# Regrouping a masked-softmax matmul: one quarter of the rows of eight batches per group, in 16 KB runs, on one Trainium2 core

## The chip, the cores and the metric

The kernel runs on one core of one Trainium2 chip, the others being idle. The metric is device time in microseconds; shorter is better. An execution counts as fast or slow by its state (one that is over 1.5% above the fastest of the same kernel is called slow; a single run's state is unknown), and ratios use fast runs only. A profile's span is some 1.8 us shorter than the time of the same execution.

## The reference, cut to what matters

```python
batch, m, k, n = 16, 512, 512, 512          # x: 16 x 512 x 512 float32, weight: 512 x 512 float32
mask = np.triu(np.ones((m, n))) == 0        # 1 strictly below the diagonal
y = scale * np.matmul(x, weight)
y = np.where(mask == 1, y, -1e9)
y_max = np.max(y, axis=-1, keepdims=True)
y_exp = np.exp(y - y_max)
return y_exp / np.sum(y_exp, axis=-1, keepdims=True)
```

16.8 MB come in, 16.8 MB go out. The part of a row above the diagonal is zero in the result, so products there can be left out; row 0 is masked completely and comes out as 1/512 everywhere.

## The kernel before

A group is one half (256) of the rows of two neighbouring batches. A partition holds four neighbouring rows, 8 KB, as one run, in input and output. HBM side: 64 row sets (`p`) of 2 batches (`e`).

```python
x_r = x.rearrange("(c e) (h p t) k -> c h p e (t k)", e=2, h=2, t=T)        # T = 4
out_r = out.rearrange("(c e) (h p t) n -> c h p e (t n)", e=2, h=2, t=T)

def load(u):
    xf = x_pool.tile([P, T, K], FP32, name="xf")                            # 8 buffers
    seq(nc.sync.dma_start(xf.rearrange("p t k -> p (t k)"), x_r[u // 2, u % 2]))
# ... cast to bf16 (VectorE), 16 transposes (TensorE), eviction (VectorE and ScalarE) ...
def multiply(u):                                                            # cut
    NC = (h + 1) * HB                                                       # 256 or 512 columns
    for t in range(T):
        for kt in range(KT):
            seq(nc.tensor.matmul(py[:, :NC], lhsT=xt[:, kt, t], rhs=w_bf[:, kt, :NC], ...))
        seq(nc.tensor.matmul(py[:, h * HB : NC], lhsT=ident_bf, rhs=band[:, h, t], ...))   # adds the mask
        seq(nc.scalar.activation(out=ot[:, t, :NC], in_=py[:, :NC], func=AF.Exp, accum_out=...))
# ... normalise (VectorE) ...
def store(u):
    seq(nc.sync.dma_start(out_r[u // 2, u % 2], ot.rearrange("p t n -> p (t n)")))
```

`band` is the mask spread over the partitions by eight products and eight copies before the loop.

The softmax here doesn't subtract the row's maximum and nothing guards it: scores larger than these inputs give would overflow.

## Time and profile before

| | before |
|---|---|
| time, median of 4 runs | 90.53 us (90.43 to 90.63) |
| span of the profile | 88.8 us |
| moved | 34.87 MB in 37 transfers; 4224 packets of 8 KB, 512 of 512 bytes |
| TensorE busy | 71.3 us |

The main lines of this profile stand in the prediction. Beside them, these from the page's list of transfers (what is moved, queue, count, KB each, median us from issue to landing):

```profile
xf<-in_x_dram SPq DMA_DIRECT2D x16, 1024.0 KB, 13.7
out_dram<-ot SPq DMA_DIRECT2D x16, 1024.0 KB, 11.9
```

A load of 1 MB needs 2.5 us at 425 GB/s. That it lands 13.7 us after its issue means that it stands in a queue behind others. While such a queue stood, the 16 transfer engines were full: a share of 0.99 to 1.04 in the stretches from 12 to 85 us. (A packet is one record of the trace and here one run: 4224 of 8 KB are 33 transfers of 128 runs. The share of transfer time, below, is the time of the packets over that of 16 engines; a packet counts where it starts, so a stretch can pass 1.)

### The profile page before, as it was taken

What the parts mean: (1) busy time and instruction counts of PE and PEld (TensorE: products, weight loads), DVE (VectorE), ACT (ScalarE), POOL (GpSimd) and SP (SyncE); (2) the same over time, 40 slices, a digit from 0 to 9 for tenths busy, and PEclk for the clock granted to TensorE, in tenths of its full rate; (3) what the DMA queues carried; (4) which work ended last, traced back from release to release, by engine and by line L of the source; (5) the groups of instructions that cost most, each with busy time, mean ns of one, the idle gap of its engine ahead of it and who ended that gap; (6) DMA issues with size and microseconds to landing.
All of it is one profiled execution on the core that took longest, in us unless ns stands there. A gap on an engine that the chain in (4) does not pass through costs nothing.

```text
span 88.8 us, 1632 instructions
## 1 busy us (share of the span) xinstructions
PE 71.3 (80%) x596; PEld 49.3 (56%) x596; DVE 60.6 (68%) x124; ACT 55.2 (62%) x154; POOL 7.3 (8%) x20
## 2 busy tenths in 40 slices
PE   4984409999999999999999999999999999800000
PEld 1324109875795598479659857965895695300000
DVE  5866485479799779949986987976594998070000
ACT  5401461887797686969777787977778786710000
POOL 7620000002001000200010020002000202000000
PEclk9999655899999999999999999999999999997555
DMA  0899999999999999999999999999999999999970
GB/s 15 306 373 384 381 376 428 417 432 428 414 425 417 425 436 428 402 417 432 428 428 417 428 421 421 425 436 425 421 417 432 425 421 425 428 432 428 425 306 26
DMA packets 5334, 34.95 MB, mean 394 GB/s; under 512 B 592, under 2 KB 1104, under 8 KB 1104
## 3 DMA queue, kind: packets, MB, share of 16 engines
q1 hardware_dynamic: 5328, 34.87, 94.6%
q8 instruction: 4, 0.07, 0.3%
q14 instruction: 2, 0.02, 0.0%
HBM read 18.09 MB, written 16.78 MB: 393 GB/s over the span
## 4 chain that ended last, share of the span: by engine, by line
PE 72%; DMA 10%; DVE 3%; SPq 2%; ACT 1%; DVEq 0%; issue 0%; ACTq 0%
PE py L116 47%; PE pt L92 16%; DMA xf<-in_x_dram 10%; PE py L125 8%; DVE ot L152 1%; DVE xb L83 1%; SPq L163 1%; SPq L78 1%; ACT ot L135 1%; PE py L215 0%; SPq L167 0%; DVEq L284 0%; DVE rinv L150 0%; ACTq L284 0%
## 5 line engine op out<-in xcount | busy, mean ns | idle before, releaser
L116 PE MATMUL py<-w_bf,xt 128*128 128x256 bf16 (+1 forms) x256 | 50.0, 329 | 0.0
L135 ACT ACTIVATE ot<-py 128x256 f32<-128x256 f32 (+1 forms) x64 | 31.2, 493 | 7.5 <-PE py L125 7.1
L116 PEld LDWEIGHTS <-xt 128*128 128x128 bf16 x256 | 24.8, 99 | 12.2
L103 ACT COPY xt<-pt 128x1024 bf16<-128x1024 bf16 x16 | 16.2, 1012 | 12.9 <-PE pt L92 8.8
L152 DVE TENSOR_SCALAR ot<-ot,rinv 128x256 f32<-128x256 f32 (+1 forms) x64 | 23.5, 431 | 0.8
L83 DVE CAST xb<-xf 128x2048 bf16<-128x2048 f32 x16 | 19.5, 1220 | 5.0 <-DMA xf<-in_x_dram 5.0
L92 PE MATMUL pt<-ident_bf,xb 128*128 128x128 bf16 x256 | 17.8, 225 | 3.7 <-DVE xb L83 3.7
L92 PEld LDWEIGHTS <-xb 128*128 128x128 bf16 x256 | 16.6, 115 | 5.8 <-DVE xb L83 4.9
L125 PE MATMUL py<-band,ident_bf 128*128 128x256 bf16 x64 | 17.6, 275 | 0.0
L102 DVE COPY xt<-pt 128x1024 bf16<-128x1024 bf16 x16 | 11.0, 687 | 6.2 <-PE pt L92 6.2
L135 ACT ACTIVATION_READ_ACCUMULATOR ot<-py 128x1 f32 x64 | 12.8, 200 | 0.0
L154 POOL MEMSET ot<- 2x256 f32 x8 | 3.6, 448 | 65.7 <-DVE ot L152 65.7
L125 PEld LDWEIGHTS <-ident_bf 128*128 128x128 bf16 x64 | 6.3, 99 | 4.2
L180 PE MATMUL py<-zeros 128*128 128x512 bf16 x12 | 5.2, 619 | 1.2 <-DVE zeros L177 1.2
L150 DVE RECIPROCAL rinv<-rsum 128x4 f32<-128x4 f32 x16 | 2.7, 168 | 2.8 <-ACT ot L135 2.8
L186 DVE MEMSET ot<- 128x1024 f32 x4 | 3.6, 912 | 0.6 <-issue 0.6
L180 PEld LDWEIGHTS <-zeros 128*128 128x128 bf16 x12 | 1.6, 144 | 3.9 <-issue 2.8
L226 DVE CAST band<-py 64x256 bf16<-64x256 f32 x4 | 1.6, 414 | 2.5 <-PE py L215 2.5
L215 PE MATMUL py<-diag_bf,spread 128*128 128x256 bf16 x8 | 1.6, 339 | 1.2 <-DVE diag_bf L202 1.2
L226 ACT CAST band<-py 64x256 bf16<-64x256 f32 x4 | 1.4, 367 | 1.4 <-DVE band L226 1.4
L193 ACT ACT_TABLE_LOAD x1 | 1.3, 1283 | 0.7 <-PEq L270 0.7
L215 PEld LDWEIGHTS <-spread 128*128 128x128 bf16 x8 | 0.9, 111 | 1.5 <-issue 1.3
(14 smaller groups left out, 7.5 us busy)
## 6 DMA issues: line engine op xcount, KB each, us to landing
xf<-in_x_dram SPq DMA_DIRECT2D x16, 1024.0 KB, 13.7
out_dram<-ot SPq DMA_DIRECT2D x16, 1024.0 KB, 11.9
w_f<-in_weight_dram SPq DMA_DIRECT2D x1, 1024.0 KB, 7.0
diag_f<-in_mask_dram SPq DMA_DIRECT2D x4, 64.0 KB, 7.7
```

The costliest lines, as they stand in the source:

```text
L83: seq(nc.vector.tensor_copy(xb, st_x.pop(u)))
L92: nc.tensor.transpose(st_pt[u][kt // 2][:, kt % 2, t], xb[:, t].rearrange("p (k kt) -> p kt k", kt=KT)[:, kt], ident_bf,)
L102: seq(nc.vector.tensor_copy(xt[:, 0:2], pt[0]))
L103: seq(nc.scalar.copy(xt[:, 2:4], pt[1]))
L116: nc.tensor.matmul(py[:, :NC], lhsT=xt[:, kt, t], rhs=w_bf[:, kt, :NC], start=(kt == 0), stop=(kt == KT - 1),)
L125: nc.tensor.matmul(py[:, h * HB : NC], lhsT=ident_bf, rhs=band[:, h, t], start=False, stop=True, skip_group_check=True,)
L135: nc.scalar.activation(out=ot[:, t, :NC], in_=py[:, :NC], func=AF.Exp, bias=0.0, scale=float(scale), accum_out=rsum[:, t : t + 1],)
L152: seq(nc.vector.tensor_scalar_mul(ot[:, t, :NC], ot[:, t, :NC], rinv[:, t : t + 1]))
L154: seq(nc.gpsimd.memset(ot[0:2, 0, :HB], 1.0 / N))
L180: seq(nc.tensor.matmul(idle, lhsT=zeros[:, :P], rhs=zeros, start=True, stop=True))
L186: nc.vector.memset(ots[i][:, :, HB:], 0.0)
L226: seq(copy(band[half, h, t : t + 2, g * P : (g + 1) * P], src[half, :, g]))
```

## The change

Its intent: longer runs (16 KB) and fewer, larger transfers; products only up to the diagonal block of 128 columns; the mask block multiplied as loaded, through a matrix that picks its rows, in place of the spread `band`. The core of the diff, with cuts:

```diff
+S = 8
+T = 4
+X_BUFS = 5
...
-    x_r = x.rearrange("(c e) (h p t) k -> c h p e (t k)", e=2, h=2, t=T)
-    out_r = out.rearrange("(c e) (h p t) n -> c h p e (t n)", e=2, h=2, t=T)
+    x_r = x.rearrange("(c e) (q p t) k -> c q p e (t k)", e=E, q=Q, t=S)      # E = 8, Q = 4
+    out_r = out.rearrange("(c e) (q p t) n -> c q p e (t n)", e=E, q=Q, t=S)
...
-        NC = (h + 1) * HB
+        NC = (q + 1) * P
...
-                    py[:, h * HB : NC],
-                    lhsT=ident_bf,
-                    rhs=band[:, h, t],
+                    py[:, q * P : NC],
+                    lhsT=spread[:, slots(u)][:, t],
+                    rhs=diag_bf[:, q],
...
+            if g in (0, G - 1):
+                store(g, slots(u - 1))
+            elif part == R - 1:
+                store(g)
```

The HBM side of a transfer now has 16 row sets (`p`) of 8 batches (`e`). The loads of x and the stores share this shape.

More of the change, by code (lines that the diff above doesn't have):

```diff
@@ L15 @@
 P = 128
-X_BUFS = 8
-OUT_BUFS = 8
-WARM = 12
+S = 8
+T = 4
+X_BUFS = 5
 @with_exitstack
@@ L45 @@
     K2, N = weight.shape
-    assert K == K2 and N == 512 and K == 512 and M == 512 and B % 2 == 0
+    assert K == K2 and N == 512 and K == 512 and M == 512 and B % S == 0
     KT = K // P
-    T = 4
-    HP = P // 2
-    HB = 2 * P
-    U = B
+    E = S
+    Q = M // P
+    R = S // T
+    OUT_BUFS = 8 * T // S
+    G = B // E * Q
+    U = G * R
     const = ctx.enter_context(tc.tile_pool(name="const", bufs=1))
@@ L65, with quarter, slots, load @@
     w_bf = const.tile([P, KT, N], BF16, name="w_bf")
-    diag_f32 = const.tile([P, KT, P], FP32, name="diag_f32")
-    diag_bf = const.tile([P, KT, P], BF16, name="diag_bf")
-    spread = const.tile([P, T, P], BF16, name="spread")
+    diag_f32 = const.tile([P, Q, P], FP32, name="diag_f32")
+    diag_bf = const.tile([P, Q, P], BF16, name="diag_bf")
+    spread = const.tile([P, S, P], BF16, name="spread")
     zeros = const.tile([P, N], BF16, name="zeros")
-    band = const.tile([P, 2, T, HB], BF16, name="band")
-    ots = [const.tile([P, T, N], FP32, name=f"ot{i}") for i in range(OUT_BUFS)]
+    ots = [const.tile([P, S, N], FP32, name=f"ot{i}") for i in range(OUT_BUFS)]
     st_x, st_xb, st_pt, st_xt, st_sum = {}, {}, {}, {}, {}
     seq = tc.keep_in_program_order
-    def load(u):
-        xf = x_pool.tile([P, T, K], FP32, name="xf")
-        seq(nc.sync.dma_start(xf.rearrange("p t k -> p (t k)"), x_r[u // 2, u % 2]))
-        st_x[u] = xf
+    def quarter(g):
+        return Q - 1 - g % Q
+    def slots(u):
+        return slice(T * (u % R), T * (u % R) + T)
+    def load(g, part=slice(0, S)):
+        if g not in st_x:
+            st_x[g] = x_pool.tile([P, S, K], FP32, name="xf")
+        run = slice(part.start * K, part.stop * K)
+        seq(nc.sync.dma_start(st_x[g].rearrange("p t k -> p (t k)")[:, run], x_r[g // Q, quarter(g)][:, :, run]))
+    def load_mask(q):
+        r = slice(q * P, (q + 1) * P)
+        seq(nc.sync.dma_start(diag_f32[:, q], mask[r, r]))
     def cast(u):
         xb = xb_pool.tile([P, T, K], BF16, name="xb")
-        seq(nc.vector.tensor_copy(xb, st_x.pop(u)))
+        seq(nc.vector.tensor_copy(xb, st_x[u // R][:, slots(u)]))
         st_xb[u] = xb
@@ L104, in evict, with mask_to_bf @@
         st_xt[u] = xt
+    def mask_to_bf(q):
+        seq(
+            nc.vector.tensor_scalar(
+                out=diag_bf[:, q],
+                in0=diag_f32[:, q],
+                scalar1=-MASK_NEG,
+                scalar2=MASK_NEG,
+                op0=ALU.mult,
+                op1=ALU.add,
+            )
+        )
     def multiply(u):
-        h = u % 2
-        NC = (h + 1) * HB
+        q = quarter(u // R)
+        NC = (q + 1) * P
         xt = st_xt.pop(u)
-        ot = ots[u % OUT_BUFS]
+        ot = ots[u // R % OUT_BUFS][:, slots(u)]
         rsum = sum_pool.tile([P, T], FP32, name="rsum")
@@ L146, in normalise @@
     def normalise(u):
-        ot = ots[u % OUT_BUFS]
-        NC = (u % 2 + 1) * HB
+        q = quarter(u // R)
+        ot = ots[u // R % OUT_BUFS][:, slots(u)]
+        NC = (q + 1) * P
         rinv = sum_pool.tile([P, T], FP32, name="rinv")
@@ L152, in normalise @@
             seq(nc.vector.tensor_scalar_mul(ot[:, t, :NC], ot[:, t, :NC], rinv[:, t : t + 1]))
-        if u % 2 == 0:
-            seq(nc.gpsimd.memset(ot[0:2, 0, :HB], 1.0 / N))
-    def store(u):
-        ot = ots[u % OUT_BUFS]
-        seq(nc.sync.dma_start(out_r[u // 2, u % 2], ot.rearrange("p t n -> p (t n)")))
-    def load_mask(b):
-        r = slice(b * P, (b + 1) * P)
-        seq(nc.sync.dma_start(diag_f32[:, b], mask[r, r]))
-    load(0)
-    load_mask(0)
-    seq(nc.sync.dma_start(w_f32, weight.rearrange("(p kt) n -> p kt n", kt=KT)))
@@ L168 @@
-    load_mask(1)
-    load(1)
-    load_mask(2)
-    load(2)
-    load_mask(3)
-    for u in range(3, X_BUFS):
-        load(u)
-    nc.vector.memset(zeros, 0.0)
-    idle = psum_y.tile([P, N], FP32, name="py")
-    for _ in range(WARM):
-        seq(nc.tensor.matmul(idle, lhsT=zeros[:, :P], rhs=zeros, start=True, stop=True))
-    make_identity(nc, ident_bf)
-    nc.gpsimd.memset(band[:HP, :, :, P:], MASK_NEG)
-    nc.gpsimd.memset(band[HP:, :, :, :P], 0.0)
-    for i in range(0, OUT_BUFS, 2):
-        nc.vector.memset(ots[i][:, :, HB:], 0.0)
-        nc.gpsimd.memset(ots[i][0:2, 0, HB:], 1.0 / N)
@@ L190 @@
-    for g in range(2):
-        for e in range(2):
-            seq(
-                nc.scalar.copy(
-                    spread.rearrange("k t (g p e) -> k t g p e", g=2, e=2)[:, :, g, :, e],
-                    ident_bf.rearrange("k (p t) -> k t p", t=T),
-                )
-            )
-    def spread_mask(h):
-        blocks = slice(2 * h, 2 * h + 2)
-        seq(
-            nc.vector.tensor_scalar(
-                out=diag_bf[:, blocks],
-                in0=diag_f32[:, blocks],
-                scalar1=-MASK_NEG,
-                scalar2=MASK_NEG,
-                op0=ALU.mult,
-                op1=ALU.add,
-            )
-        )
-        for t in range(0, T, 2):
-            pm = psum_y.tile([P, N], FP32, name="py")
-            for j in range(2):
-                seq(
-                    nc.tensor.matmul(
-                        pm[:, j * HB : (j + 1) * HB],
-                        lhsT=spread[:, t + j],
-                        rhs=diag_bf[:, blocks].rearrange("k b c -> k (b c)"),
-                        start=True,
-                        stop=True,
-                    )
-                )
-            src = pm.rearrange("p (t g c) -> p t g c", t=2, g=2)
-            for g, copy in enumerate((nc.vector.tensor_copy, nc.scalar.copy)):
-                half = slice(g * HP, (g + 1) * HP)
-                seq(copy(band[half, h, t : t + 2, g * P : (g + 1) * P], src[half, :, g]))
@@ new lines, in normalise, with store @@
+        if q == 0 and u % R == 0:
+            seq(nc.gpsimd.memset(ot[0:E, 0, :P], 1.0 / N))
+    def store(g, part=slice(0, S)):
+        run = slice(part.start * N, part.stop * N)
+        ot = ots[g % OUT_BUFS].rearrange("p t n -> p (t n)")
+        seq(nc.sync.dma_start(out_r[g // Q, quarter(g)][:, :, run], ot[:, run]))
+    load(0, slots(0))
+    seq(nc.sync.dma_start(w_f32, weight.rearrange("(p kt) n -> p kt n", kt=KT)))
+    load_mask(Q - 1)
+    if R > 1:
+        load(0, slots(1))
+    for g in range(1, X_BUFS):
+        load(g)
+        if g < Q:
+            load_mask(quarter(g))
@@ new lines, with spin @@
+    nc.vector.memset(zeros, 0.0)
+    def spin(n):
+        idle = psum_y.tile([P, N], FP32, name="py")
+        for _ in range(n):
+            seq(nc.tensor.matmul(idle, lhsT=zeros[:, :P], rhs=zeros, start=True, stop=True))
+    spin(9)
+    make_identity(nc, ident_bf)
+    seq(
+        nc.scalar.copy(
+            spread.rearrange("k t (p e) -> k t p e", e=E),
+            ident_bf.rearrange("k (p t) -> k t p", t=S).unsqueeze(3).to_broadcast([P, S, P // S, E]),
+        )
+    )
+    for i in range(OUT_BUFS):
+        NC = (quarter(i) + 1) * P
+        if NC < N:
+            nc.gpsimd.memset(ots[i][:, :, NC:], 0.0)
+        if NC == P:
+            nc.gpsimd.memset(ots[i][0:E, 0, NC:], 1.0 / N)
@@ L228 @@
     cast(0)
     transpose(0)
+    spin(3)
     evict(0)
-    spread_mask(0)
     seq(nc.vector.tensor_copy(w_bf[:, 0:2], w_f32[:, 0:2]))
     seq(nc.scalar.copy(w_bf[:, 2:4], w_f32[:, 2:4]))
+    mask_to_bf(Q - 1)
     cast(1)
     for u in range(U + 1):
+        if u == 0:
+            multiply(0)
         if u + 1 < U:
             transpose(u + 1)
-        if u == 0:
-            evict(1)
+            evict(u + 1)
         if u + 2 < U:
             cast(u + 2)
-        if 0 < u < U - 1:
-            evict(u + 1)
-        if u < U:
+        if 0 < u < U:
+            if u % R == 0 and u // R < Q:
+                mask_to_bf(quarter(u // R))
@@ L246 @@
             multiply(u)
-        if u == 0:
-            spread_mask(1)
         if u >= 1:
+            g, part = divmod(u - 1, R)
             normalise(u - 1)
-            store(u - 1)
-            if u - 1 + X_BUFS < U:
-                load(u - 1 + X_BUFS)
+            if g in (0, G - 1):
+                store(g, slots(u - 1))
+            elif part == R - 1:
+                store(g)
+            if part == R - 1 and g + X_BUFS < G:
+                load(g + X_BUFS)
 _INS = ['x', 'weight', 'scale', 'mask']
```

## The prediction

(The cost of a packet, 8.2 ns, is an estimate from the medians of two sizes in the trace before.)

> **What bounds the kernel now.** I started at the page, at the busy shares by slice, because two resources look full at once: TensorE and the transfers.
>
> ```profile
> span 88.8 us, 1632 instructions
> ...
> PE   4984409999999999999999999999999999800000
> ...
> DMA  0899999999999999999999999999999999999970
> GB/s 15 306 373 384 381 376 428 417 432 428 414 425 417 425 436 428 402 417 432 428 428 417 428 421 421 425 436 425 421 417 432 425 421 425 428 432 428 425 306 26
> ...
> q1 hardware_dynamic: 5328, 34.87, 94.6%
> ```
>
> A slice is 2.22 us. TensorE is full from slice 8 to slice 35 and then idle for five slices. The 16 transfer engines are full from the second slice to the last but one, also in those five. The queue moves 34.87 MB; at the 425 GB/s of the middle slices that alone is 82.0 us of the 88.8. The rest is the empty start, some loss in the first 12 us and the tail. I therefore asked for busy time in chosen stretches:
>
> ```profile
> 2.00:4.00 2.00, 2.00 (x6) 0.76 (x5) 1.68 (x3) 0.98 (x5) 1.65 (x4) 1.00 0.81 254
> ...
> 8.00:10.00 2.00, 0.84 (x12) 0.66 (x10) 0.98 (x2) 1.01 (x1) 0.00 (x0) 0.87 0.95 344
> 10.00:12.00 2.00, 0.72 (x4) 0.17 (x2) 1.43 (x3) 1.13 (x3) 0.00 (x0) 0.50 0.91 360
> ...
> 40.00:60.00 20.00, 20.00 (x187) 14.79 (x185) 17.04 (x36) 16.33 (x47) 0.90 (x2) 1.00 1.01 425
> ...
> 82.00:84.00 2.00, 0.00 (x0) 0.00 (x0) 0.00 (x0) 0.00 (x0) 0.00 (x0) 0.50 1.01 426
> ...
> 85.00:86.00 1.00, 0.00 (x0) 0.00 (x0) 0.00 (x0) 0.00 (x0) 0.00 (x0) 0.50 0.74 311
> 86.00:87.00 1.00, 0.00 (x0) 0.00 (x0) 0.00 (x0) 0.00 (x0) 0.00 (x0) 0.50 0.33 139
> ```
>
> The last two figures of a line are the share of transfer time and the GB/s. From 12 us to 85 us nothing but the transfer rate counts. From 85.3 to 87 us some engines are done and others still have a packet or five.
>
> The chain that ended last is nearly all TensorE (72% of the span), which would suggest that faster products shorten the kernel. It ends at 80 us, though, with the last normalisation. What comes after is in SyncE's waits and in its timeline:
>
> ```profile
> SPq L158 <- DVE ot L152: 49.8, 15, 9.6
> SPq L284 <- DMA out_dram<-ot: 7.1, 2, 4.7
> ```
>
> The last store is issued near 80.0 us and SyncE then waits 7.1 us for stores. One store is 1.05 MB, 2.5 us at 425 GB/s. So about 4.6 us of older transfers still stood in the queue: compute came 4.6 us before it would have let the queue run dry. The kernel is bound by the transfers, with compute a close second. Making compute shorter is worth nothing by itself.
>
> [...] In this trace's packet records the median 8192-byte packet takes 309 ns, the 512-byte one (mask) 27 ns, the 4-byte one (semaphore) 9 ns. A line through the first two has a slope of 282 ns / 7680 B = 0.0367 ns/B, which is 16 / 0.0367 = 436 GB/s, and an intercept of 8.2 ns, which the 9 ns of the 4-byte packet confirms. [...] This kernel already alternates between two batches 1 MiB apart and runs at 425[...].
>
> **The change part by part.** *Bytes.* Nothing is removed: whole x, whole output, weight and four 64 KB mask blocks, 34.87 MB again.
>
> *Packets.* Before: 128 per load and store of 8 KB, 32 x 128 = 4096, with the weight 4224, and 512 of the mask. After: loads of seven groups and stores of six go in 16 KB runs, 13 x 128 = 1664 packets; the first group's load and the first and last groups' stores are halved, 6 x 128 = 768 packets of 8 KB; the weight has 128; the mask 512. That is 1664 fewer. By the line above a 16 KB packet should take 8.2 + 602 = 610 ns instead of 2 x 309 = 618. Saved: 1664 x 8.2 ns / 16 engines = 0.85 us. All of it is on the path, as the queue is full all the time. Transfers drop from 37 to 24, so 13 x 16 = 208 semaphore packets of 9 ns go: 0.12 us.
>
> *Mask bursts.* The stretches 8:10 and 10:12 have shares of 0.95 and 0.91, and in the packet records the engines' share falls to 0.7 to 0.9 exactly while 512-byte packets pass (around 5.5, 8.3 and 11.4 us), a loss of about 0.36 us in all; the fourth burst, at 14.2 us, loses nothing. I take it that a burst costs when it is near the front of the queue. After the change one burst comes behind the weight, near 8 us; the others come behind 2 MB loads, at some 16, 21 and 26 us (estimates at 425 GB/s). I credit 0.2 us.
>
> *TensorE.* From the chain in order of time, four 512-wide products take 0.86 us, four 256-wide 0.44, a 256-wide mask product 0.11, sixteen transposes 0.89. A unit of 512 columns takes 0.89 + 4 x 0.97 = 4.8 us, one of 256 takes 0.89 + 4 x 0.55 = 3.1, times eight each: 63 us. After, the widths are 512, 384, 256 and 128 with a 128-wide mask product (0.055): units of 4.6, 3.7, 2.9 and 2.0 us, four each: 53 us. Ten us less, none of it on the path to the end. The old preparation of the mask (8 products, 8 copies) goes too; it lay before 20 us, beside full transfers.
>
> *VectorE and ScalarE.* Casts (1.22 us) and evictions (0.69 and 1.01 us) stay at 16 each. Four normalisations take 1.27 us at 256 columns and 1.68 at 512, so by line 1.07 at 128 and 1.48 at 384: 5.5 us for the four widths, times four 22.0, where it was 8 x 2.95 = 23.6. VectorE then needs some 3.5 us per unit and now sets compute's pace. The transfers need 2 x 1.05 MB / 425 = 4.9 us per unit. Compute stays faster.
>
> *Does the queue ever run dry?* Now 11.25 MiB of loads are issued ahead (10 of x) where it was 9.25 (8 of x), so the queue lasts from 2.2 to about 30 us. The first store needs the cast of the fourth half-group first in VectorE's order, whose data land near 16 us: it should be issued near 19 to 20 us, 10 us before need (before: 22.2 us). Then queue positions, at 4.9 us per 2 MiB group: first store done 35, load 5 at 40, store 1 at 45, load 6 at 50, store 2 at 54, load 7 at 59, store 3 at 64, then stores 4, 5, 6 at 69, 74, 79. The last group writes into the output buffer that store 3 frees, at 64 us; two units of at most 3.5 us later its stores are issued, near 72 us. They are needed at 79. So the queue stays fed, with a margin of about 7 us, against 4.6 now.
>
> Sum: 0.85 + 0.12 + 0.2 = 1.17 us. The span goes from 88.8 to 87.6 and the time from 90.6 to 89.4, a gain of 1.3%.
>
> **Rivals.** (a) *The products were the bound*: the chain names TensorE, and 10 us less would give about 80 us. Against it: the transfers are at 0.99 or more to 85 us with 34.87 MB to move, so 82 us is a floor. (b) *The new address pattern is slow*[...]. [...]even a twentieth of the rate costs 4 us: 94.5. [...] Against it: [...]the pitch of 1 MiB is there already. (c) *A new wait starves the queue*: 2 MB steps and four large output buffers instead of eight. If the last group came 3 us late, 92. Against it: the 7 us margin. (d) *The fixed cost doesn't shrink*: long runs are cut into 8 KB pieces, or a 16 KB packet takes 618 ns: 90.3. (e) *The tail shrinks as well*: the 85.3 to 87 us stretch holds about 0.8 us of idle engine time; were it gone with the rest, 88.6, just over 2% faster.
>
> **Range and chances.** The known gain is 1 to 1.2 us; (d) puts the upper end at 90.4, (e) the lower at 88.7. Crossing 2% faster takes 88.8, which needs nearly the whole tail: 0.11. Slower by 2% (above 92.4) needs (b) or (c): 0.05. Within 2%: 0.84.
>
> **What would show it.** Right: transfer queue bytes 34.87 MB in some 3500 packets, 16 KB packets near 610 ns, the middle stretches near 429 GB/s, TensorE busy much less with gaps inside, SyncE's last wait longer than 7.1 us. Wrong: a slice under 400 GB/s between 15 us and 83 us (starved, if the share of transfer time falls too; slow HBM, if the share stays full and packets take longer); packets still at 8 KB; or the middle at 425 with a shorter tail.

## The result and the profile after

Ratios here and below are the mean time of one kernel's fast runs over that of the other's of the same rounds, so they are not quite the ratio of the medians quoted.

The changed kernel takes 132.44 us (131.16 to 133.73, 4 runs, the longest of them slow) against 90.53: ratio 1.458, 95% interval 1.446 to 1.470. It is correct, and 46% slower. I had predicted 89.4 and a range of 88.7 to 90.4. The profile is of a fast run. Its page:

```profile
span 129.4 us, 1562 instructions
PE 72.3 (56%) x588; PEld 49.6 (38%) x588; DVE 52.8 (41%) x118; ACT 50.3 (39%) x147; POOL 6.9 (5%) x12
...
DMA  3999999899998999999999999999999999999620
GB/s 86 238 361 257 233 223 243 182 243 213 213 238 187 238 203 208 294 403 306 223 228 410 360 228 223 355 431 238 218 329 426 390 390 395 365 352 339 233 81 23
...
q1 hardware_dynamic: 3456, 34.87, 93.9%
...
DMA 72%; PE 5%; DVE 4%; SPq 1%; issue 1%; ACT 1%; DVEq 0%; ACTq 0%
...
xf<-in_x_dram SPq DMA_DIRECT2D x7, 2048.0 KB, 33.8
```

The engines are as full as before (a 9 in nearly every slice), the bytes are the same 34.87 MB, but the rate is 180 to 260 GB/s for long stretches where it was 425. The queue is not starved: the engines are busy and slow (a share of 1.01 at 216 GB/s from 30 to 50 us). (Summed in the packet records and divided by 16 engines, packets took 121.5 us, 84.0 before: that is 37.5 of the 40.6 us by which the span grew.) The chain is now transfers (72%), and compute waits for them. TensorE's busy time did not fall although a sixth of its work is gone. It idles between loads, and its mean granted clock was 0.78 where it had been 0.92; the same products take 59.8 us at 0.91 in a later run with fast loads. The same in stretches (share of transfer time and GB/s are the last two figures):

```profile
12.00:30.00 18.00, 10.17 (x60) 5.57 (x59) 6.01 (x9) 5.84 (x12) 0.00 (x0) 0.69 1.05 228
30.00:50.00 20.00, 16.42 (x135) 11.29 (x134) 11.31 (x25) 11.85 (x35) 0.00 (x0) 0.86 1.01 216
53.00:58.00 5.00, 2.08 (x26) 1.96 (x24) 3.29 (x9) 1.95 (x7) 0.00 (x0) 0.79 0.98 385
...
98.00:102.00 4.00, 2.85 (x22) 2.54 (x23) 3.96 (x8) 0.88 (x1) 0.00 (x0) 0.50 1.03 434
```

Up to 50 us only loads move (x, after the weight and with the masks), at half the rate. The first two stores go from 52 to 58 us, and around 100 us stores alone run at the full 434. In the packet records a 16 KB packet took 1240 ns (median) between 14 and 50 us, all loads, and 611 between 95 and 106 us, nearly all stores. My 610 ns came true for these late stores, and the loads took twice that. At 220 instead of 430 GB/s, 16.8 MB of x cost 76 us instead of 39. These 37 us are most of the 42 that were lost.

### The profile page after: what moved, and what is told of

Its sections match the earlier page's. It is cut to its first block, busy times and chain, and to the rows that moved or that the text cites. A ratio compares the mean times of both kernels' runs of the same rounds, so it can differ in the third digit from the quotient of the medians.

```text
span 129.4 us, 1562 instructions
## 1 busy us (share of the span) xinstructions
PE 72.3 (56%) x588; PEld 49.6 (38%) x588; DVE 52.8 (41%) x118; ACT 50.3 (39%) x147; POOL 6.9 (5%) x12
## 3 DMA queue, kind: packets, MB, share of 16 engines
q1 hardware_dynamic: 3456, 34.87, 93.9%
## 4 chain that ended last, share of the span: by engine, by line
DMA 72%; PE 5%; DVE 4%; SPq 1%; issue 1%; ACT 1%; DVEq 0%; ACTq 0%
DMA xf<-in_x_dram 65%; DMA w_f<-in_weight_dram 7%; PE py L144 2%; PE pt L108 2%; DVE ot L181 2%; DVE xb L99 2%; ACT ot L163 1%; SPq L91 1%; SPq L188 0%; PE py L153 0%; DVE rinv L179 0%; SPq L95 0%; DVEq L284 0%; DVE diag_bf L124 0%; DVEq L181 0%
## 5 line engine op out<-in xcount | busy, mean ns | idle before, releaser
L144 PE MATMUL py<-w_bf,xt 128*128 128x512 bf16 (+3 forms) x256 | 48.7, 337 | 0.3 <-ACT ot L163 0.3
L108 PE MATMUL pt<-ident_bf,xb 128*128 128x128 bf16 x256 | 21.6, 252 | 27.7 <-DVE xb L99 27.7
L163 ACT ACTIVATE ot<-py 128x512 f32<-128x512 f32 (+3 forms) x64 | 27.7, 443 | 16.7 <-PE py L153 15.8
L144 PEld LDWEIGHTS <-xt 128*128 128x128 bf16 x256 | 23.8, 109 | 20.2 <-issue 13.3
L108 PEld LDWEIGHTS <-xb 128*128 128x128 bf16 x256 | 19.3, 125 | 30.2 <-DVE xb L99 29.6
L181 DVE TENSOR_SCALAR ot<-ot,rinv 128x512 f32<-128x512 f32 (+3 forms) x64 | 20.4, 383 | 0.6
L153 PE MATMUL py<-diag_bf,spread 128*128 128x128 bf16 x64 | 15.1, 236 | 6.5 <-DVE diag_bf L124 6.5
L153 PEld LDWEIGHTS <-spread 128*128 128x128 bf16 x64 | 6.9, 108 | 4.3 <-issue 1.8
L220 POOL MEMSET ot<- 128x1024 f32 (+2 forms) x3 | 5.4, 1805 | 0.0
L212 ACT COPY spread<-ident_bf 128x1024 bf16<-128x1024 bf16 x1 | 1.0, 1045 | 0.2 <-POOL ident_bf masks.py:199 0.2
```

The costliest lines, as they stand in the source:

```text
L108: nc.tensor.transpose(st_pt[u][kt // 2][:, kt % 2, t], xb[:, t].rearrange("p (k kt) -> p kt k", kt=KT)[:, kt], ident_bf,)
L153: nc.tensor.matmul(py[:, q * P : NC], lhsT=spread[:, slots(u)][:, t], rhs=diag_bf[:, q], start=False, stop=True, skip_group_check=True,)
L181: seq(nc.vector.tensor_scalar_mul(ot[:, t, :NC], ot[:, t, :NC], rinv[:, t : t + 1]))
L212: nc.scalar.copy(spread.rearrange("k t (p e) -> k t p e", e=E), ident_bf.rearrange("k (p t) -> k t p", t=S).unsqueeze(3).to_broadcast([P, ...
L220: nc.gpsimd.memset(ots[i][:, :, NC:], 0.0)
```

## The experiments

Twelve kernels were run on three chips, each beside runs of the kernel before on its chip (medians of 90.58 to 90.77 us). Where one time is given it is a single run, of unknown state.

### First question: place in HBM, size of packet, or company?

**Loads alone.** One buffer, one 2 MB load after another from different places, each waiting for the last:

```diff
+    seq(nc.sync.dma_start(buf, one))      # 128 adjoining runs
+    seq(nc.sync.dma_start(buf, two))      # 64 row sets of 2 batches
+    seq(nc.sync.dma_start(buf, four))     # 32 row sets of 4 batches
+    seq(nc.sync.dma_start(buf, m1))       # 16 runs at each of 8 places 1 MiB apart: the change
+    seq(nc.sync.dma_start(buf, m1_16k))   # the same, 1 MiB + 16 KB apart; then + 64 KB, + 256 KB, 2 MiB, 512 KiB
+    seq(nc.sync.dma_start(buf, k256))     # 256 KiB apart: 2 MB in one piece, dealt 16 by 8
+    ...                                   # 8 KB runs; then the eight places as eight loads
```

> A kernel with no compute and a wrong result on purpose: one 2 MB load after another into one buffer, each waiting for the one before, so each has the 16 transfer engines to itself. All have 128 runs of 16 KB into 128 partitions; what differs is where the runs lie in HBM. Theory A (pitch: runs that the engines read at the same time lie a large power of two apart and collide in HBM): the contiguous load takes about 610 ns a packet and 430 GB/s; two batches 1 MiB apart about the same; eight places 1 MiB apart 1150 to 1250 ns, about half the rate, as in the changed kernel, also with runs of 8 KB (550 to 620 ns); eight places 1 MiB + 256 KB apart, or + 64 KB, near 610 to 700 ns again; 2 MiB apart as slow or slower. Theory B (a 16 KB packet into one partition is slow by itself): every 16 KB load takes 1100 to 1250 ns, the contiguous one too, and the 8 KB one 309. Theory C (loads collide with stores or with compute): every load here runs at 610 ns.

Its stretches, for four batches, the change's pattern, 1 MiB + 16 KB apart, and the piece of 2 MB that adjoins (columns: length, GpSimd busy, clock, transfer share, GB/s):

```profile
26.00:30.00 4.00, 0.00 (x0) 1.00 1.05 434
34.00:42.00 8.00, 0.00 (x0) 1.00 0.92 197
46.00:54.00 8.00, 0.00 (x0) 1.00 0.93 197
...
106.00:114.00 8.00, 0.00 (x0) 1.00 0.93 205
```

All of A, B and C fail. A 16 KB packet is fast (median 611 ns) for the contiguous load, for two and for four batches. It is slow (1220 to 1262) for eight places at every distance, also where they adjoin and the transfer covers one contiguous 2 MB. So it is neither the pitch nor the size of the packet, and there was no store or compute to collide with. Eight loads of 16 partitions each were as slow, 1224 ns.

**Stores alone**, to the same places of the output.

```diff
-    seq(nc.sync.dma_start(buf, m1))
+    seq(nc.sync.dma_start(m1, buf))
```

> The mirror image, stores of a zeroed buffer to the same places of the output, one after another, wrong result on purpose. In the changed kernel's trace the 16 KB packets of the last 30 us, which are nearly all stores, take 620 to 750 ns. Theory A as it stands (HBM itself collides, whatever the direction) expects 1100 ns or more for eight places 1 MiB apart here too; theory A for reads alone expects 611 to 700 ns for all of them. Theory B expects slow 16 KB packets everywhere, theory C full rate everywhere.

615 ns for one, two and four batches and 1227 to 1229 for eight places at every distance. The direction doesn't matter either, for a transfer by itself. That stores ran at full rate late in the changed kernel needed another explanation.

**Half loads.**

```diff
+        if part is None:
+            load(g, slice(0, T))
+            load(g, slice(T, S))
```

> The changed kernel with every 2 MB load cut into two of 1 MB, so that its packets are of 8 KB as in the kernel before, from the same addresses in the same groups of eight batches. Theory A: still 125 to 140 us, packets of loads near 550 to 620 ns. Theory B: the loads are back at 309 ns a packet and the time falls to 89 to 95 us. Theory C: no change, 125 to 140.

128.93 us, one run; its 8 KB packets took 624 ns (median, 10 to 50 us) against 309 before. The size of the packet is out in the full kernel too.

**Four batches.**

```diff
-S = 8
+S = 4
-X_BUFS = 5
+X_BUFS = 10
```

> The changed kernel with 4 instead of 8 batches in a group (its own parameter: 4 rows a run, 8 KB, four places 1 MiB apart, ten input buffers); compute is that of the change. Theory A: collisions shrink with the number of places, so between 89 and 105 us, with load packets of 309 to 400 ns; if four places don't collide at all, 89 to 91 us. Theory B: 8 KB packets, so 89 to 91 us. Theory C: still above 120 us, since compute and the mix of loads and stores stay.

91.08 us (90.65 to 91.15), ratio 1.004 (1.001 to 1.007), packets of 309 ns. Everything of the change but the eight batches, the 16 KB runs and the 2 MB transfers is here, and the loss is gone. What the change saved in compute brings nothing, as the transfers bind.

### Second question: is it the side of the partitions?

What all slow transfers share is 16 row sets of 8, one set to 8 neighbouring partitions (1220 to 1262 ns a packet alone, 611 for 64 sets of 2 and 32 of 4). Theory D below supposes that the loss arises on this side of a transfer: it comes with the way the runs are spread over the partitions, wherever they lie in HBM, and only while the engines go through such a pattern in step; with some of them ahead of the others it should go away. How engines could hinder each other there was a supposition of mine that no run shows; D is judged only by what follows from it. (The packet records name neither the engine nor the partition, so which engine fills which partitions, and which engines are ahead of others, isn't shown either. I rebuilt the sequences of packets below by joining each packet to one that starts where it ends.)

**Loads divided.**

```diff
+    seq(nc.sync.dma_start(buf, places(16, 8, 9)))     # run number 9 p + e
+    seq(nc.sync.dma_start(buf, places(32, 4, 5)))
+    seq(nc.sync.dma_start(buf, places(64, 2, 3)))
+    seq(nc.sync.dma_start(buf, runs[0:128]))
+    seq(nc.sync.dma_start(buf[0:64], runs[0:64]))                                            # partitions 0 to 63
+    seq(nc.sync.dma_start(buf.rearrange("(p two) f -> two p f", two=2)[0], runs[0:64]))     # 0, 2, 4, ...
+    # three loads as in the change, then the two small ones, then three more
+    seq(nc.sync.dma_start(b4[0:16], places(4, 4, 5)))
+    seq(nc.sync.dma_start(b4[16:64], places(12, 4, 5)))
```

> Loads alone again, wrong result on purpose. The earlier run of loads alone refuted the pitch: eight places were slow at every distance, even when they adjoin (256 KB, one piece of 2 MB), and 16 KB packets were fast when contiguous. Theory D[...]. Theory E (HBM after all: what counts is which runs are read at one moment, not a pitch). Parts 1 to 4, the same 2 MB to 2.3 MB of HBM with a gap after each group[...]: 16 groups of 8 (150 KB apart, no power of two), 32 of 4, 64 of 2, 128 contiguous. D: 1150 to 1260 ns, then 611 three times. E: no reason for the first to be slow, all near 611. Parts 5 and 6, the same 1 MB of HBM into partitions 0 to 63, then into every other partition of 128. D: 1200 ns, then 611. E: the same for both. Parts 7 to 12: three loads of the changed kernel's pattern in a row, then two small loads[...], then three more of the pattern, with no wait between. D: 1240 ns a packet before, and after the small loads[...], mostly 611 to 700 ns. E: 1240 before and after.

The stretches: 16 by 8; 32 by 4; partitions 0 to 63; every other partition; the change's pattern in a row; the same after the two small loads.

```profile
4.00:12.00 8.00, 0.00 (x0) 1.00 0.95 203
16.00:21.00 5.00, 0.00 (x0) 1.00 0.85 364
...
40.00:43.00 3.00, 0.00 (x0) 1.00 0.91 186
47.00:49.00 2.00, 0.00 (x0) 1.00 0.92 393
56.00:86.00 30.00, 0.00 (x0) 1.00 1.00 215
92.00:100.00 8.00, 0.00 (x0) 1.00 1.01 395
```

The medians are 1244, 611, 611, 611 (contiguous), 1265, 611 ns, as D expects. The pair of partitions 0 to 63 and every other partition is the clearest: the same 1 MB of HBM, the same 64 runs, and only the partitions differ. The last two lines are the other test. The pattern is the same in both, and only the two small loads came between, which were meant to put some engines ahead of others. (Which runs are read at one moment changes with that too, so against E the pair of partitions counts for more.) One engine's packets, in ns, in order:

```
... 1253 1271 1279 1087 1136 1255 1273 1035 | 614 619 612 841 615 619 612 805 619 612 615 808 619 612 615
```

Left of the bar are packets before the small loads, right of it packets after them. There every fourth takes 805 to 841 ns; why, no run shows. E fails.

### Third question: is that all of the loss in the kernel?

**Loads in a row**, **stores in a row** and **both in a row**: the changed kernel with contiguous runs on one side or both. Their outputs are wrong, which doesn't matter for the times.

```diff
-    ..., x_r[g // Q, quarter(g)][:, :, run]))
+    ..., x.rearrange("b (r s) k -> (b r) (s k)", s=S)[g * P : (g + 1) * P, run]))
-    seq(nc.sync.dma_start(out_r[g // Q, quarter(g)][:, :, run], ot[:, run]))
+    seq(nc.sync.dma_start(out.rearrange("b (r s) n -> (b r) (s n)", s=S)[g * P : (g + 1) * P, run], ot[:, run]))
```

> The changed kernel with the loads of x from 128 contiguous runs of 16 KB instead of 16 groups of 8; stores, compute and all waits as in the change, so the result is wrong on purpose. Theory D, with loads as the whole of the loss: load packets 611 ns and 88 to 93 us, stores at 611 to 700 ns though they still go out in 16 groups of 8. If the stores cost their half as they do alone, about 110 us.

> The other half: the changed kernel with its loads as they are and the stores to 128 contiguous runs, wrong result on purpose. If the loads are the whole of the loss, 122 to 133 us as the change (16.8 MB of loads at 220 GB/s are 76 us, the other 18.1 MB at 425 are 43, with 5 to 7 us of start and end). If stores cost as much as loads, about 110.

> The changed kernel with both loads and stores as 128 contiguous runs of 16 KB (wrong result on purpose); same bytes, packets, issues, waits and compute as the change. It asks whether anything but the way of the runs over engines and partitions was wrong in my prediction. Theory D alone: 89.4 us, as I predicted for the change (88.9 to 90.2), 16 KB packets at 611 ns. If 2 MB steps, four output buffers or the order of the groups cost something of their own, 91 to 96.

Loads in a row: 98.15 us. Stores in a row: 125.34. Both: 89.93 (89.75 to 90.24), ratio to before 0.993 (0.990 to 0.995). Loads in a row and stores in a row are single runs. So of the 132.44 the way of the loads costs about 34.3 us and that of the stores about 7.1, each undone alone; undone together they give back 42.5, all of the loss and the small gain beside it. 98.15 is above my 88 to 93: the stores are not free, though far from the 110 of half rate. From the page of both in a row:

```profile
span 88.5 us, 1559 instructions
PE 59.8 (68%) x585; PEld 42.7 (48%) x588; DVE 52.9 (60%) x118; ACT 49.5 (56%) x147; POOL 7.9 (9%) x12
...
GB/s 59 319 422 408 445 422 398 417 430 341 407 428 432 415 415 419 470 422 393 445 430 415 430 430 422 437 422 437 430 415 430 430 415 452 415 433 407 426 204 19
```

Large steps, four output buffers and the order of the groups starve nothing: from the third slice to the third from the end only one is under 390 (341, while mask packets pass).

**Stores in line**, four stores of the pattern from a standing start, two loads, four stores:

```diff
+    for q in range(4):
+        seq(nc.sync.dma_start(out_r[0, q], buf))
+    # ... two loads of the same pattern ...
+    for q in range(4):
+        seq(nc.sync.dma_start(out_r[1, q], buf))
```

> Stores of the changed kernel's pattern alone, wrong result on purpose: four in a row from a standing start, then two loads of the pattern, then four more stores. In the changed kernel's trace stores ran at 309 ns (8 KB) and mostly 611 (16 KB) once in a row, although single stores took the double. Theory D[...]: after the first 8 to 16 packets most fall to 611 ns, with a slow one every fourth. If stores don't do so by themselves: 1230 ns throughout.

The start, and the stretch behind the loads (here with VectorE's and GpSimd's busy time):

```profile
7.00:11.00 4.00, 0.00 (x0) 0.00 (x0) 1.00 0.97 197
...
46.00:60.00 14.00, 0.00 (x0) 0.00 (x0) 1.00 1.01 430
```

One engine's packets from the standing start:

```
1279 1279 1265 1408 611 980 1269 1519 611 611 1146 1491 611 611 855 1485 611 611 611 1468 611 611 611 1148 611 611 611
```

Stores of this pattern get faster by themselves: the first four packets take 1265 to 1408 ns, of the last twelve only every fourth is slow (1485, 1468, 1148; the sequences of other engines are less regular). Behind loads they were at 611 after about eight packets, without a slow fourth. Loads did not do this: in the changed kernel the median was 1240 ns from 14 to 50 us. D would have it that engines fall out of step when they send; neither that, nor why loads stay slow, is shown by a run here.

**Staggered** and **staggered later**: correct kernels, the change with one issue cut in two, meant to put some engines ahead of others (that it does is not shown). In the first it is the very first load; in the later one, weight and masks come first and this is the next:

```diff
-    if R > 1:
-        load(0, slots(1))
+    for rows in (slice(0, 4), slice(4, 16)):
+        seq(nc.sync.dma_start(st_x[0].rearrange("p t k -> p (t k)")[rows.start * E : rows.stop * E, T * K :],
+                              x_r[0, quarter(0)][rows, :, T * K :]))
```

> The changed kernel, correct, with one issue of its 24 cut in two: the very first 1 MB load goes as rows of 4 groups and of 12 groups[...]. Theory D: most load packets fall to 611 to 700 ns and the time to 90 to 100 us[...]. Theory E or any other that blames addresses, packet size or compute: 125 to 135 us as before.

> The stagger once more, correct result. The first try put it at the very first load, with the weight[...], and the mask between it and the stream[...]. Now weight and all masks come first and the second half of the first group's load is the one cut in rows of 4 and 12 groups, directly ahead of the 2 MB loads. Theory D: the loads 1 to 4 that follow show fours of one packet near 800 to 900 ns and three near 615 (as in the loads alone), so they end near 30 us instead of 50, and the time is 95 to 118 us, depending on how long the offset lasts once stores come between. If the offset has no effect in the full kernel, 130 to 134.

The first failed: 132.76 us, which by what was expected speaks against D, with 1152 ns (median) from 14 to 50 us. After the cut load its 8 KB packets mostly took 310 to 950 ns in no order. I read this as the weight, issued next, meeting the cut load, so that what the cut had set apart was lost at once; I had overlooked it, no run shows it by itself, and the later run tests the reading. It took 105.43 us, 27 us less than the change by the cut of one issue and an earlier place for the masks, with the same bytes (no run separates the two). In its stretch of loads 1 to 4 the median is 615 ns:

```profile
20.00:30.00 10.00, 5.26 (x37) 4.12 (x39) 5.62 (x8) 2.02 (x2) 0.00 (x0) 0.54 0.99 419
```

There was no 800 in every fourth, better than expected. But load 4 landed at 40.0 us (55.0 in the change), not near 30 as expected: from 12 to 18 us the rate was still 191 GB/s. Later loads, which come between stores, were slow again in part (299 and 287 GB/s in the packet records of the stretches from 46 and from 58 us), which with a slow start leaves it at 105.

### A candidate

**Halves of four**: 16 KB runs, four batches, half of the rows (32 row sets of 4), with two mask products per row set.

```diff
-    E = S
-    Q = M // P
+    E = 4
+    Q = 2
...
+            for half in range(2):
+                seq(nc.tensor.matmul(py[:, q * HB + half * P : NC], lhsT=spread[:, half, slots(u)][:, t], ...))
```

> A correct candidate: runs of 16 KB as in the change, but a group is one half of the rows of FOUR neighbouring batches[...]; products up to the end of the half as before the change; the mask as it was loaded, by two products per row set (256 and 128 wide). Theory D: all 16 KB packets at 611 ns, 89.0 to 90.3 us, a gain of about 0.85 us over before from the packets' fixed cost, if compute (64 more 128-wide products, 3.5 us of TensorE) stays ahead of the queue; if it does not, 91 to 93.

91.98 us (six runs; the four fast ones 91.87 to 91.98, two slow ones to 93.74), ratio 1.014 (1.013 to 1.016). The packets are at 611, and it loses all the same, for the second of the reasons expected. Its profile fell in the slow state, so only the place of the loss is read from it:

```profile
74.00:78.00 4.00, 3.95 (x40) 2.96 (x39) 2.58 (x7) 3.02 (x8) 0.00 (x0) 1.00 0.56 233
78.00:82.00 4.00, 3.78 (x39) 3.22 (x36) 2.49 (x8) 3.36 (x16) 0.45 (x1) 1.00 0.47 197
```

Transfers are busy for half the time only, while TensorE (first figure) is full: its last stores came too late. That the fast runs lose in the same place is not shown. No correct kernel here beats the one before. Both in a row (wrong) gained 0.7%, in part by a faster start (next section).

## Why the prediction was wrong

- **The bound**: right. The queue binds before and after, and 10 us less of TensorE work gave nothing (four batches, 91.08).
- **Bytes, packets, the 16 KB packet**: right away from the slow pattern. 34.87 MB, 3456 packets, and medians of 611 to 615 ns for 610 predicted, in every contiguous, two- and four-batch transfer over the 128 partitions.
- **The step that failed** is that I took the rate of the new pattern for unchanged. All 16 engines did work (transfer share 1.01). I took this for the full rate and never asked which partitions the runs then fill. That this side counts is shown by the same 64 runs at 1265 ns into partitions 0 to 63 and at 611 into every other one; by what mechanism is not. The term of the sum that I left at zero is 1240 instead of 611 ns for most packets of x, about 34 us, and some 7 us more for the stores.
- **Rival (b)** named the right suspect, the new pattern, and looked at the wrong end of the transfer: at the pitch in HBM, which changed nothing (1220 to 1262 ns at every distance), instead of the partitions. So did my argument against it ("the pitch of 1 MiB is there already"). Its size, 4 us, was a guess at a twentieth where the loss was half (and 94.5 is 4 us on the old time, not on the 89.4).
- **Queue never dry, rivals (c) and (d)**: right. The share of transfer time is about 1 to 118 us; both in a row excludes the step size, half loads the packet. In both in a row the first store was issued at 21.7 us (19 to 20 predicted), the last at 73.2 (72), and SyncE's last wait was 13.9 us, longer than 7.1 as predicted. **Rival (e)** did not come: there the share was 0.53 from 84 to 86 us and 0.16 to 87, against 0.74 and 0.33 from 85 to 87 before.
- **The small gain**: without the slow packets, 0.74 us were gained (both in a row, 90.67 to 89.93) of 1.17 predicted, and that it comes so near is in part luck. Contiguous loads were issued faster (the first in 0.37 us, 0.67 before and in the change), and the first packet moved at 1.75 us, 2.18 in those two. In the packet records this run was 0.37 MB ahead of the kernel before at 10 us and 0.36 MB at 80 us, so its lead at the end is no more than that of its start. Between 30 and 80 us a 16 KB packet took 616.7 ns on average and two of 8 KB 621.6: 4.9 ns saved and not 8.2, which for 1664 packets is an estimate of 0.5 us instead of 0.85. The mask bursts are unclear: the engines' idle time between 4 and 30 us fell from about 0.4 to 0.2 us, as credited, but the 512-byte packets took 32 ns on average, 28 before. The rest of the difference I can't assign.
- **Slips of reading that change nothing**: TensorE was full from slice 7 to slice 34. The old margin was overread: only 2.57 MB started after 80.0 us, 1.05 of them the last store's own, which leaves 3.6 us of older transfers; the wait of 7.1 us holds the landing too.
- **"TensorE busy much less"**: wrong in the changed kernel (72.3 against 71.3 us, at a mean granted clock of 0.78 against 0.92); right once loads were fast (59.8, at 0.91).

## What to carry to other kernels

When an access pattern is regrouped, look at how a transfer's runs lie on the partitions, not only in HBM, and run its shape by itself before counting packets or bytes: here 16 sets of 8 took 1244 ns a packet where 32 of 4 took 611. "All 16 engines busy" in a profile is compatible with half the rate (a share of 1.01 at 216 GB/s). Read the share of busy time and the GB/s together, and the time of one packet: here a full share at half the rate was slow packets (1240 instead of 611 ns), not a wait of the queue. A bare kernel of single transfers, one per suspected shape, told more in one run than the full kernel could.
